# Gating tables requested behind the gate blocks, and tiles that share buffers, in a two-layer hybrid encoder

## The chip, the cores and the metric

The kernel runs on one core of one Trainium2 chip. The metric is the device time of one launch in microseconds (us), as the median of several runs. Beside it stands one profiled execution, whose instructions the hardware profiler recorded with their start, their duration and the semaphores that they waited for.

The engines have short names in the rows: PE is TensorE's matrix multiply and PEld its loading of stationary weights, DVE is VectorE, ACT is ScalarE, POOL is GpSimd, and SP is SyncE, which only issues transfers here. Each engine works off its instructions in program order.

## The reference

There are 256 tokens of width 2048 and two layers. Everything is float32.

```
for l in range(2):
    h = rms_norm(x, norm1_g[l])
    q, k, v, gu, gv = split(h @ w_in[l])                  # 1024 | 256 | 256 | 1024 | 1024
    q, k = rope(rms_norm(q per head)), rope(rms_norm(k per head))
    attn = softmax(q k^T / sqrt(128), |i-j| <= 128, learned sink) v   # 8 query heads, 2 key heads
    vn   = layer_norm(gelu(gv)) * sgu_ln_g + sgu_ln_b
    f    = w_s[head] @ vn  (per chunk of 128 tokens) + b_s
    sgu  = gelu(gu) * f
    x = x + concat(rms_norm(attn), rms_norm(sgu)) @ w_o[l]
    g, u = split(depthwise_conv3(rms_norm(x) @ w_up[l]))  # 2 x 5632
    x = x + (silu(g) * u) @ w_down[l]
```

## The kernel before

**Products.** Every float32 operand of a large product is split in two float32r parts: hi, a rounded copy that ACT makes (L128), and lo, the rest, that DVE makes by a subtraction (L112). A product is then three matmuls (hi with hi, hi with lo, lo with hi). The weights come from HBM in blocks of 128 x 2048 (1 MB), each by one transfer that SP issues (L120), into one of 3 buffers `raw`; hi and lo of half a block lie in one of 4 buffers each. A transfer into `raw` waits until DVE has made the last lo of the block that lay there, so SP runs three blocks ahead of that subtraction, and ACT and DVE run up to two blocks ahead of PE.

**Stages of a layer.** The input projection takes 20 blocks of `w_in` in chunks of 4 (keys and values, queries of head group 0, queries of head group 1, two chunks for `gv`), 24 matmuls a block (L168). Then `gu` is made in four gate units of two blocks of `w_gu` each (`unit`, 32 matmuls at L209 and 32 short ones at L214), then come `w_o`, the up projection and the down projection.

**Attention beside it.** The work of the two head groups is written as two generators (`attend`) whose steps are taken between blocks of the projection and in the gate units: a query row is scaled, squared and rotated; its rows are cut into 16-bit halves by ACT (`apart`, L422), sent through the transposing transfer (`sent`, L429, four transfers for a group, two more for the keys), put together again by ACT (`together`, L435) and split in hi and lo (`parts`, L302 and L303). Then follow the scores (`matmul3`, L308 to L310, 128 x 256), a masked reading of them by DVE (L498), exponentials on ACT (L520), the division (L528), transposes of the probabilities on PE (L536), another split and the products with the values (L308 to L310, 128 x 512). The scores and these transposes write into two PSUM buffers `tp`.

**Gating.** `gating_tables` requests eight tables of 256 KB: two of `w_s` (L408) and six rows of `prow`, each copied to all 128 partitions (L413): two of the gain, two of the offset, two of `b_s`. `normal` applies gain (L769) and offset (L770) on DVE to the normalised `gv` (L768). `spatial` multiplies with `w_s` on PE (L751) and adds `b_s` on DVE (L762).

**What sets the order.** A scheduler places each engine's instructions ahead of time. Code under `urgent()` comes as early as it can, other code in written order as its inputs are expected; `take` lets a step begin behind the latest PE instruction written so far. Most tiles, also the tables, come from one pool of 43 general buffers (`sl`), and a request waits, in the scheduler's plan and on the chip, for the last reader of what lay in its buffer. The query rows have 4 buffers `q`.

Of the kernel before, what the change touches and what calls it, by code (L numbers as in the profile page):

```python
# [8 lines left out]
F32 = mybir.dt.float32  # L9
F32R = mybir.dt.float32r  # L10
U16 = mybir.dt.uint16
AF = mybir.ActivationFunctionType
ALU = mybir.AluOpType
AX = mybir.AxisListType

P = 128
# [4 lines left out]
HD = 128  # L21
# [6 lines left out]
W = 512  # L28
# [14 lines left out]
def encoder(ctx: ExitStack, tc: tile.TileContext, xT, x, w_in, w_gu, w_o, w_up, w_down, wsT, pcol, prow, rope, out):  # L43
    nc = tc.nc
    pool = lambda name, bufs, **kw: ctx.enter_context(tc.tile_pool(name=name, bufs=bufs, **kw))
    const = pool("const", 1)
    lay = pool("lay", 2)
    slots = pool("slots", 43)
    rowp = pool("rowp", 4)
    evp = pool("evp", 4)  # L50
    rawp = pool("rawp", 3)
# [7 lines left out]
    def sl(shape, dt=F32):  # L59
        return slots.tile(shape, dt, tag="sl", name="sl")  # L60

    def row(tag):
        return rowp.tile([P, W], F32, tag=tag, name=tag)

    def ev():
        return evp.tile([P, 2, SEQ], F32, tag="ev", name="ev")
# [4 lines left out]
    def st(shape, tag):  # L71
        return small.tile(shape, F32, tag=tag, name=tag)
# [4 lines left out]
    def tp(shape):  # L77
        return tpp.tile(shape, F32, tag="tp", name="tp")
# [4 lines left out]
    def urgent():  # L83
        return tc.high_priority(offset=AHEAD)
# [215 lines left out]
    def parts(src, shape):  # L300
        hi, lo = sl(shape, F32R), sl(shape, F32R)
        nc.scalar.activation(hi, src, AF.Copy)  # L302
        nc.vector.tensor_tensor(out=lo, in0=src, in1=hi.bitcast(F32), op=ALU.subtract)  # L303
        return hi, lo
# [100 lines left out]
    def gating_tables(l):  # L405
        ws = [sl([P, 4, P]) for _ in range(2)]
        for i in range(2):
            nc.sync.dma_start(ws[i], wsT[l, :, 4 * i : 4 * i + 4, :])  # L408
        rows = []
        for r0 in (R_LG, R_LB, R_BS):  # L410
            for i in range(2):
                t = sl([P, W])
                nc.sync.dma_start(t, prow[l : l + 1, r0 + i * W : r0 + (i + 1) * W].partition_broadcast(P))  # L413
                rows.append(t)
        return ws, rows


    def apart(srcs):
        halves = []
        for src in srcs:  # L420
            h = sl([P, 2, 2 * P], U16)
            nc.scalar.copy(h, src.bitcast(U16).rearrange("p (n b) -> p b n", b=2))  # L422
            halves.append(h)
        return halves

    def sent(halves):
        tall = sl([P, 4, SEQ], U16)
        for m in range(2):
            nc.sync.dma_start_transpose(tall[:, :, m * P : (m + 1) * P], halves[m].rearrange("p b n -> p (b n)"))  # L429
        return tall  # L430

    def together(tall):
# [33 lines left out]
    def attend(g, ps, r, kT, v, tab, qk, nsink, acc, pc, outs):  # L466
        ms = st([P, 2, 4], "qms")
        rot = []
        for m in range(2):
            q = row("q")  # L470
            with urgent():
                nc.scalar.activation(q, ps[:, m, :], AF.Copy, scale=r[:, m : m + 1])
            head_squares(q, 4, ms[:, m, :])
            rot.append(rotate(q, m, 4, tab))
        qr = inv_rms(ms.rearrange("p a b -> p (a b)"), HD, "q", 8)
        qs = st([P, 8], "qs")
        nc.vector.tensor_scalar_mul(qs, qr, HD**-0.5)
        rows = [rot[m].rearrange("p h d -> p (h d)") for m in range(2)]
        halves = [apart([rows[m][:, h : h + 2 * HD] for m in range(2)]) for h in (0, 2 * HD)]
        yield  # L480
        talls = [sent(h) for h in halves]
        yield
        qT = []
        for tall in talls:
            pq = parts(together(tall), [P, 2, SEQ])
            qT += [[v[:, i, :] for v in pq] for i in range(2)]
        yield
        scores = []
        for pr in range(2):
            nmx = st([P, 2, 2], "nmx")  # L490
            for i in range(2):
                h = 2 * pr + i
                t = tp([P, 2, SEQ])
                s = sl([P, 2, SEQ])
                for m in range(2):
                    matmul3(t[:, m, :], [v[:, m * P : (m + 1) * P] for v in qT[h]], [v[:, g, :] for v in kT])
                for m in range(2):
                    nc.vector.tensor_tensor_reduce(  # L498
                        out=s[:, m, :],
                        in0=t[:, m, :],  # L500
                        in1=mask[:, m, :],
                        scale=qs[:, 4 * m + h : 4 * m + h + 1],
                        scalar=LOWEST,
                        op0=ALU.add,
                        op1=ALU.max,
                        accum_out=nmx[:, i, m : m + 1],
                    )
                scores.append(s)
            h0 = 4 * g + 2 * pr
            sink = qk[:, R_SINK + h0 : R_SINK + h0 + 2].unsqueeze(2).to_broadcast([P, 2, 2])  # L510
            nsk = nsink[:, h0 : h0 + 2].unsqueeze(2).to_broadcast([P, 2, 2])
            nm = st([P, 2, 2], "nm")
            nc.vector.scalar_tensor_tensor(out=nm, in0=nmx, scalar=-1.0, in1=nsk, op0=ALU.mult, op1=ALU.min)
            es = st([P, 2, 2], "es")
            nc.vector.tensor_tensor(out=es, in0=nm, in1=sink, op=ALU.add)
            rs = st([P, 2, 2], "rs")
            for i in range(2):
                s = scores[2 * pr + i]
                for m in range(2):
                    nc.scalar.activation(s[:, m, :], s[:, m, :], AF.Exp, bias=nm[:, i, m : m + 1], accum_out=rs[:, i, m : m + 1])  # L520
            nc.scalar.activation(es, es, AF.Exp)
            nc.vector.tensor_tensor(out=rs, in0=rs, in1=es, op=ALU.add)
            rec = st([P, 2, 2], "rec")
            nc.vector.reciprocal(rec, rs)
            for i in range(2):
                s = scores[2 * pr + i]
                for m in range(2):
                    nc.vector.tensor_scalar_mul(s[:, m, :], s[:, m, :], rec[:, i, m : m + 1])  # L528
            yield
        for pr in range(2):  # L530
            pT = []
            for b in range(2):
                t = tp([P, 2, SEQ])
                for i in range(2):
                    for m in range(2):
                        nc.tensor.transpose(  # L536
                            t[:, i, m * P : (m + 1) * P], scores[2 * pr + i][:, m, b * P : (b + 1) * P], ident
                        )
                pT.append(parts(t.rearrange("p a b -> p (a b)"), [P, W]))
            yield  # L540
            t = tp([P, W])
            for b in range(2):
                matmul3(t, [w[:, g * HD : (g + 1) * HD] for w in v[b]], pT[b], b == 0, b == 1)
            o = sl([P, 2, SEQ])
            nc.scalar.copy(o.rearrange("p a b -> p (a b)"), t)
            add_squares(acc, o, g == 0 and pr == 0)
            outs.extend(gained([o], C_AG + 4 * g + 2 * pr, pc))
            yield
# [9 lines left out]
        out=mask[:, 0, P:], in_=mask[:, 0, P:], compare_op=ALU.is_ge, fill=MASKED,  # L558
# [3 lines left out]
        out=mask[:, 1, :P], in_=mask[:, 1, :P], compare_op=ALU.is_ge, fill=MASKED,  # L562
# [60 lines left out]
    for l in range(DEPTH):  # L623
# [39 lines left out]
        kv = []  # L663
        for m in range(2):
            t = sl([P, W])
# [6 lines left out]
        for m in range(2):  # L672
            a = rotate(kv[m][:, : 2 * HD], m, 2, tabs[1])
            nc.vector.tensor_tensor(
                out=a, in0=a, in1=rk[:, 2 * m : 2 * m + 2].unsqueeze(2).to_broadcast([P, 2, HD]), op=ALU.mult
            )
            krot.append(a)
        vs = [parts(kv[m][:, 2 * HD :], [P, 2 * HD]) for m in range(2)]
        kT = []

        khalves = apart([a.rearrange("p h d -> p (h d)") for a in krot])
# [2 lines left out]
        def sent_keys():  # L684
            ktall.append(sent(khalves))
# [20 lines left out]
        r1b = as_rows(r1)  # L706
        second = group_steps(1, ps)
        second()
        ws, lrows = gating_tables(l)


        vn = []
# [1 line left out]
        for i in range(2):  # L714
            if l:
                between = [[[first], [first], [], [first]], [[first, second], [first], [second, first], [second]]]
            else:
                between = [[[first], [first], [first], [second]], [[second], [], [first], [first]]]
            ps = chunk(3 + i, between[i])
            for m in range(2):  # L720
                t = row("vn")
                with urgent():
                    nc.scalar.activation(t, ps[:, m, :], AF.Copy, scale=r1[:, m : m + 1])
                nc.scalar.activation(t, t, AF.Gelu_apprx_tanh)
                nc.vector.bn_stats(out=stats[:, m, i, :], in_=t)
                vn.append(t)
        mv = st([P, 2, 2], "mv")
        for m in range(2):
            nc.vector.bn_aggr(out=mv[:, m, :], in_=stats[:, m, :, :])
# [116 lines left out]
        for f0, f1 in ((0, 24), (24, NF)):  # L846
            ys = []
            for f in range(f0, f1, 2):
# [7 lines left out]
                t = convolved(ps2, NF + f)  # L856
# [85 lines left out]
```

## Time and profile before

| | us |
|---|---|
| median of 3 runs (lowest, highest) | 1993.09 (1992.59, 1994.17) |
| the profiled execution: its own time | 1992.69 |
| the profiled execution: span from first to last instruction | 1990.9 |
| PE busy in the span | 1985.5 |
| DVE busy, ACT busy | 1367.6, 1134.5 |

The profiled execution took 0.40 us less than the median, and 1.79 us of it lie outside the span. Matmuls are pipelined and their ends are modelled in the profile, so that PE's busy time also covers small stops; where PE stopped is read from the weight loads (PEld) that began late.

### The profile page before, as it was taken

The numbers are of one execution on the slowest core, as the hardware profiler recorded it, in microseconds if no ns is written. First come the engines' busy times: TensorE is split into PE (matmuls) and PEld (weight loads), VectorE is DVE, ScalarE is ACT, GpSimd is POOL, SyncE is SP. The second block draws the span as 40 slices with busy tenths as digits, with TensorE's granted clock in tenths as the row PEclk, the third lists the DMA queues.
The fourth block names the chain that finished last, engine by engine and source line by source line (L and its number), as shares of the span: only waits on it lengthen the run. The fifth ranks groups of instructions, "written<-read, shape, count | busy, mean of one in ns | idle before, by whom it ended". The sixth has DMA issues, their size and how long they took to land.

```text
span 1990.9 us, 26332 instructions
## 1 busy us (share of the span) xinstructions
PE 1985.5 (100%) x10292; PEld 1704.8 (86%) x10292; DVE 1367.6 (69%) x1930; ACT 1134.5 (57%) x1514; POOL 23.3 (1%) x25
## 2 busy tenths in 40 slices
PE   9999999999999999999999999999999999999999
PEld 8888888888888888888888888888888888888887
DVE  6778677777754577775566786777777445777753
ACT  6786585556543455556667675855555344555542
POOL 0100000000000000000000000000000000000000
PEclk9999999999999999999999999999999999999999
DMA  9754674455555544556767536745545554455563
GB/s 341 243 161 149 219 222 169 170 208 207 198 191 192 188 170 174 212 207 204 219 205 237 161 142 226 198 169 206 207 180 211 191 192 167 171 208 203 201 212 127
DMA packets 95580, 391.15 MB, mean 196 GB/s; under 512 B 43744, under 2 KB 45024, under 8 KB 50912
## 3 DMA queue, kind: packets, MB, share of 16 engines
q1 hardware_dynamic: 94736, 388.74, 56.6%
q8 instruction: 80, 1.31, 0.3%
q10 hardware_dynamic: 720, 0.73, 0.1%
q14 instruction: 44, 0.36, 0.1%
HBM read 378.43 MB, written 2.10 MB: 191 GB/s over the span
## 4 chain that ended last, share of the span: by engine, by line
PE 97%; ACT 1%; DVE 1%; DMA 1%; issue 0%; SPq 0%; POOL 0%; DVEq 0%; ACTq 0%
PE mm L168 42%; PE mm L234 31%; PE mm L240 16%; PE mm L209 2%; PE mm L275 1%; PE tp L168 1%; PE mm L214 1%; PE mm L270 1%; PE tp L308 0%; PE tp L751 0%; PE tp L310 0%; DVE lo L112 0%; PE tp L309 0%; DMA raw<-in_w_up 0%; ACT hi L128 0%
## 5 line engine op out<-in xcount | busy, mean ns | idle before, releaser
L112 DVE TENSOR_TENSOR lo<-raw,hi 128x1024 fp32r<-128x1024 f32 (+1 forms) x708 | 839.4, 1215 | 417.4 <-ACT hi L128 277.1
L128 ACT ACTIVATE hi<-raw 128x1024 fp32r<-128x1024 f32 (+1 forms) x708 | 730.3, 1050 | 606.8 <-PE mm L168 330.9
L168 PE MATMUL mm<-hi,sl 128*128 128x512 f32 x2480 | 667.6, 390 | 0.1
L234 PE MATMUL mm<-sl,hi 128*128 128x512 f32 x2688 | 617.8, 389 | 0.2 <-ACT hi L128 0.2
L234 PEld LDWEIGHTS mm<-sl,hi 128*128 128x128 f32 x2688 | 501.9, 188 | 103.5 <-ACT hi L128 1.1
L168 PEld LDWEIGHTS mm<-hi,sl 128*128 128x128 f32 x2480 | 464.5, 188 | 97.2 <-DVE sl L289 0.9
L168 PE MATMUL mm<-lo,sl 128*128 128x512 f32 x1240 | 382.6, 390 | 0.0
L240 PEld LDWEIGHTS mm<-sl,lo 128*128 128x128 f32 x2688 | 328.1, 192 | 3.3
L240 PE MATMUL mm<-sl,lo 128*128 128x256 f32 x2688 | 329.1, 283 | 0.0
L168 PEld LDWEIGHTS mm<-lo,sl 128*128 128x128 f32 x1240 | 232.5, 188 | 47.9
L838 DVE SCALAR_TENSOR_TENSOR sc<-ev,pc,sc 128x255 f32<-128x255 f32 x176 | 80.6, 481 | 94.0 <-ACT sc L837 94.0
L281 ACT COPY ev<-mm 128x512 f32<-128x512 f32 x96 | 55.4, 577 | 122.5 <-PE mm L240 114.8
L837 ACT ACTIVATE sc<-ev,pc 128x256 f32<-128x256 f32 x176 | 99.1, 589 | 0.0
L841 DVE SCALAR_TENSOR_TENSOR sc<-ev,pc,sc 128x255 f32<-128x255 f32 x176 | 80.6, 481 | 2.9
L296 ACT ACTIVATE sl<-sl 128x256 fp32r<-128x256 f32 x88 | 31.8, 409 | 72.8 <-DVE sl L857 72.8
L283 DVE TENSOR_TENSOR ev<-mm,ev 128x512 f32<-128x512 f32 x96 | 65.6, 683 | 0.0
L209 PE MATMUL mm<-sl,hi 128*128 128x512 f32 x256 | 61.6, 391 | 0.0
L833 DVE TENSOR_TENSOR ev<-ev,rb 128x512 f32<-128x512 f32 x88 | 60.1, 682 | 0.1
L209 PEld LDWEIGHTS mm<-sl,hi 128*128 128x128 f32 x256 | 47.3, 188 | 9.2
L289 DVE SCALAR_TENSOR_TENSOR sl<-sl,pc 128x256 fp32r<-128x256 f32 x96 | 42.6, 479 | 17.7 <-ACT sl L288 17.6
L297 DVE TENSOR_TENSOR sl<-sl 128x256 fp32r<-128x256 f32 x88 | 33.5, 422 | 19.4 <-ACT sl L296 19.4
L288 ACT ACTIVATE sl<-sl,pc 128x256 fp32r<-128x256 f32 x96 | 43.2, 497 | 1.1 <-DMA sl<-in_xT 0.9
(124 smaller groups left out, 813.2 us busy)
## 6 DMA issues: line engine op xcount, KB each, us to landing
raw<-in_w_up SPq DMA_DIRECT2D x172, 1024.0 KB, 5.2
raw<-in_w_down SPq DMA_DIRECT2D x88, 1024.0 KB, 4.9
raw<-in_w_in SPq DMA_DIRECT2D x38, 1024.0 KB, 5.1
raw<-in_w_o SPq DMA_DIRECT2D x32, 1024.0 KB, 4.9
raw<-in_w_gu SPq DMA_DIRECT2D x16, 1024.0 KB, 4.9
raw<-in_w_up SPq DMA_DIRECT2D x8, 512.0 KB, 4.5
sl<-in_prow SPq DMA_DIRECT2D x12, 256.0 KB, 7.3
raw<-in_w_in SPq DMA_DIRECT2D x8, 256.0 KB, 5.2
```

The lines of the kernel that those rows point to most:

```text
L112: nc.vector.tensor_tensor(out=lo, in0=part, in1=hi.bitcast(F32), op=ALU.subtract)
L128: nc.scalar.activation(hi[:, cs], part, AF.Copy)
L168: nc.tensor.matmul(ps[m], acts[kk][:, part % 2, m * P : (m + 1) * P], w, start=first and kk == 0 and part == 0, stop=last and kk == KB - 1 ...
L209: nc.tensor.matmul(ps[:, i, :], tile_of(his, k, i), x1, start=k == 0, stop=False)
L234: nc.tensor.matmul(pss[n][:, i, :], hs[k // KB][:, c : c + P], x1, start=k == 0, stop=False)
L240: nc.tensor.matmul(pss[n][:, i, :SEQ], los[k // KB][:, c : c + P], acts[k][:, 0, :], start=False, stop=k == len(acts) - 1)
L281: nc.scalar.copy(rest, ps[:, :, SEQ:])
L283: nc.vector.tensor_tensor(out=s, in0=ps[:, :, :SEQ], in1=rest, op=ALU.add)
L833: nc.vector.tensor_tensor(out=s, in0=s, in1=r2b2[0], op=ALU.mult)
L837: nc.scalar.activation(t[:, i, :], s[:, i, :], AF.Identity, bias=col(3), scale=col(1))
L838: nc.vector.scalar_tensor_tensor(out=t[:, i, 1:], in0=s[:, i, : SEQ - 1], scalar=col(0), in1=t[:, i, 1:], op0=ALU.mult, op1=ALU.add)
L841: nc.vector.scalar_tensor_tensor(out=t[:, i, : SEQ - 1], in0=s[:, i, 1:], scalar=col(2), in1=t[:, i, : SEQ - 1], op0=ALU.mult, op1=ALU.add)
```

## The change

Five things are changed. `gating_tables` is called behind the two `gv` chunks and no longer ahead of them. The transposing transfers of `sent` stand under `urgent()`. The hi and lo parts of a value row share one general buffer, where each had its own. The 16-bit halves of a query row for both pairs of heads are made by one ACT copy into one buffer, where there were two copies and two buffers. The query rows have 2 buffers, and the general pool has 46.

```diff
-    slots = pool("slots", 43)
+    slots = pool("slots", 46)
...
-        return rowp.tile([P, W], F32, tag=tag, name=tag)
+        return rowp.tile([P, W], F32, tag=tag, name=tag, bufs=2 if tag == "q" else 4)
...
         tall = sl([P, 4, SEQ], U16)
-        for m in range(2):
-            nc.sync.dma_start_transpose(tall[:, :, m * P : (m + 1) * P], halves[m].rearrange("p b n -> p (b n)"))
+        with urgent():
+            for m in range(2):
+                nc.sync.dma_start_transpose(tall[:, :, m * P : (m + 1) * P], halves[m].rearrange("p b n -> p (b n)"))
...
-        rows = [rot[m].rearrange("p h d -> p (h d)") for m in range(2)]
-        halves = [apart([rows[m][:, h : h + 2 * HD] for m in range(2)]) for h in (0, 2 * HD)]
+        both = []
+        for m in range(2):
+            t = sl([P, 2, 2, 2 * HD], U16)
+            words = rot[m].rearrange("p h d -> p (h d)").bitcast(U16)
+            nc.scalar.copy(t, words.rearrange("p (j n b) -> p j b n", j=2, b=2))
+            both.append(t)
+        halves = [[t[:, pr, :, :] for t in both] for pr in range(2)]
...
-        vs = [parts(kv[m][:, 2 * HD :], [P, 2 * HD]) for m in range(2)]
+        vs = []
+        for m in range(2):
+            t = sl([P, 2, 2 * HD], F32R)
+            v = kv[m][:, 2 * HD :]
+            nc.scalar.activation(t[:, 0, :], v, AF.Copy)
+            nc.vector.tensor_tensor(out=t[:, 1, :], in0=v, in1=t[:, 0, :].bitcast(F32), op=ALU.subtract)
+            vs.append([t[:, 0, :], t[:, 1, :]])
...
         second = group_steps(1, ps)
         second()
-        ws, lrows = gating_tables(l)
...
                 vn.append(t)
+        ws, lrows = gating_tables(l)
         mv = st([P, 2, 2], "mv")
```

Line numbers move: L429 becomes L430, L498 L504, L536 L542, L769 L781.

**SP, layer 0, from the first transposing transfers to the second gate unit.** Before, the tables stand between the last blocks of `w_in` and the first of `w_gu`, and the transposes of the second head group behind the third block of `w_gu`:

```order
L429 DMA_TRANSPOSE sl<-sl 128x4x128 x5
L120 DMA raw<-in_w_in 128x2048
L429 DMA_TRANSPOSE sl<-sl 128x4x128
L120 DMA raw<-in_w_in 128x2048 x2
L408 DMA sl<-in_wsT 128x512 x2
L413 DMA sl<-in_prow 128x512
L120 DMA raw<-in_w_in 128x2048
L413 DMA sl<-in_prow 128x512 x2
L120 DMA raw<-in_w_gu 128x2048
L413 DMA sl<-in_prow 128x512 x3
L120 DMA raw<-in_w_gu 128x2048 x2
```

and now all eight tables stand in one piece behind the fifth block of `w_gu`:

```order
L430 DMA_TRANSPOSE sl<-sl 128x4x128 x6
L120 DMA raw<-in_w_in 128x2048 x4
L430 DMA_TRANSPOSE sl<-sl 128x4x128 x4
L120 DMA raw<-in_w_gu 128x2048 x5
L408 DMA sl<-in_wsT 128x512 x2
L413 DMA sl<-in_prow 128x512 x6
L120 DMA raw<-in_w_gu 128x2048 x3
```

The tables moved behind five weight blocks and the transposes of group 1 ahead of all blocks of `w_gu`. In layer 1 the tables also stand behind the fifth block of `w_gu`.

**DVE, layer 0, the gain and offset.** Before, the gain (L769) comes one row at a time, between other small work, when the gate units run:

```order
L768 TENSOR_SCALAR vn<-vn,mv,lnr 128x512
L513 SCALAR_TENSOR_TENSOR nm<-nmx,nsink 128x4
L768 TENSOR_SCALAR vn<-vn,mv,lnr 128x512
L515 TENSOR_TENSOR es<-nm,qk 128x4
L769 TENSOR_TENSOR vn<-vn,sl 128x512
L303 TENSOR_TENSOR sl<-tp,sl 128x512
L770 TENSOR_TENSOR vn<-vn,sl 128x512
L769 TENSOR_TENSOR vn<-vn,sl 128x512
```

and now the gain stands ahead of the four score readings (L504) of head group 1, which free the two buffers `tp`, and of the next lo parts (L112):

```order
L743 TENSOR_SCALAR lnv<-mv 128x2
L780 TENSOR_SCALAR vn<-vn,mv,lnr 128x512 x4
L781 TENSOR_TENSOR vn<-vn,sl 128x512 x3
L504 ISA sl,nmx<-tp,mask,qs 128x256
L504 ISA nmx 128x1
```

The first two instructions of L781 read the first row of `prow` and the third reads the second row. In layer 1 DVE's order is alike, with these three instructions ahead of two score readings, the division and four lo parts.

**PE, layer 1, the first gate units.** Before, the value products of group 0 (L308 to L310, 128x512) and its scores of group 1 (128x256) stand inside the first units:

```order
L209 MATMUL mm<-sl,hi 128x512 x32
L214 MATMUL mm<-sl,lo 128x256 x10
L308 MATMUL tp<-sl 128x512
L309 MATMUL tp<-sl 128x512
L310 MATMUL tp<-sl 128x512
L308 MATMUL tp<-sl 128x512
L214 MATMUL mm<-sl,lo 128x256 x4
L309 MATMUL tp<-sl 128x512
L310 MATMUL tp<-sl 128x512
L214 MATMUL mm<-sl,lo 128x256 x8
L308 MATMUL tp<-sl 128x256
L309 MATMUL tp<-sl 128x256
```

and now group 0 is through before the units begin, and a unit and a half lie between the last scores of group 1 (the first row) and what follows on them (L542):

```order
L310 MATMUL tp<-sl 128x256
L214 MATMUL mm<-sl,lo 128x256 x30
L209 MATMUL mm<-sl,hi 128x512 x32
L214 MATMUL mm<-sl,lo 128x256 x2
L542 MATMUL tp<-ident,sl 128x128 x8
L214 MATMUL mm<-sl,lo 128x256 x30
L209 MATMUL mm<-sl,hi 128x512 x24
```

The steps of attention stand in whole groups of 6, 8 or 12 now, at the places where they are written. Over both layers PE has the same instructions as before; its order differs only from the first scores to the products with `w_o` in each layer. ACT loads its function tables 14 times in the program, and did so 17 times before.

## Rows read from the trace of the kernel before

**Rows 1.** The page: span, share of the engines, and the clock granted to PE in 40 equal slices (9 is 90% or more of full speed).

```profile
span 1990.9 us, 26332 instructions
PE 1985.5 (100%) x10292; PEld 1704.8 (86%) x10292; DVE 1367.6 (69%) x1930; ACT 1134.5 (57%) x1514; POOL 23.3 (1%) x25
...
PEclk9999999999999999999999999999999999999999
```

**Rows 2.** The chain of work that ended last, in order of time: start in us, duration in us, what; 64 long and 64 short matmuls of the up projection.

```profile
312.62 14.53 PE mm L234 x64
327.15 7.67 PE mm L240 x64
```

**Rows 3.** Waits of the weight loads in layer 0 from 74.91 to 208.93 us, grouped: who waited for whom, us in total, times, longest.

```profile
PEld tp L308 <- issue: 0.8, 2, 0.6
PEld tp L336 <- issue: 0.5, 1, 0.5
PEld mm L168 <- DVE sl L289: 0.4, 1, 0.4
PEld tp L536 <- DVE sl L528: 0.3, 1, 0.3
PEld tp L536 <- ACT sl L545: 0.2, 1, 0.2
PEld mm L168 <- ACT sl L288: 0.2, 1, 0.2
```

**Rows 4.** The same view of layer 1, from 1064.36 to 1196.53 us.

```profile
PEld mm L168 <- DVE sl L289: 0.6, 2, 0.4
PEld tp L310 <- DVE sl L303: 0.5, 1, 0.5
PEld tp L536 <- ACT sl L545: 0.5, 2, 0.3
PEld tp L536 <- DVE sl L528: 0.4, 2, 0.2
PEld tp L308 <- DVE nmx L498: 0.4, 1, 0.4
PEld tp L308 <- DVE sl L303: 0.3, 1, 0.3
PEld tp L308 <- ACT sl L302: 0.2, 1, 0.2
PEld tp L308 <- ACT sl L545: 0.2, 1, 0.2
```

**Rows 5.** The time line of the weight loads, those that began late: start, duration, instruction, and in brackets the idle time before and what ended it. The first two are of layer 0, the last four of layer 1.

```profile
115.94 0.47 PEld L536 LDWEIGHTS tp<-ident,sl 128*128 128x128 f32 x4 [0.34 <-DVE sl L528]
126.58 0.19 PEld L308 LDWEIGHTS tp<-sl 128*128 128x128 f32 x1 [0.59 <-issue]
...
1093.41 0.19 PEld L308 LDWEIGHTS tp<-sl 128*128 128x128 f32 x1 [0.35 <-DVE nmx L498]
...
1106.98 0.19 PEld L308 LDWEIGHTS tp<-sl 128*128 128x128 f32 x1 [0.34 <-DVE sl L303]
1110.69 0.42 PEld L536 LDWEIGHTS tp<-ident,sl 128*128 128x128 f32 x4 [0.32 <-ACT sl L545]
...
1130.46 0.19 PEld L310 LDWEIGHTS tp<-sl 128*128 128x128 f32 x1 [0.54 <-DVE sl L303]
```

**Rows 6.** Busy time (and instructions) of PE, PEld, DVE, ACT and POOL, granted clock, DMA share and GB/s in two stretches of layer 0.

```profile
113.00:119.00 6.00, 6.00 (x32) 4.75 (x30) 4.55 (x12) 5.95 (x14) 0.00 (x0) 1.00 0.89 230
119.00:127.00 8.00, 7.80 (x35) 6.20 (x34) 3.90 (x7) 7.58 (x10) 0.00 (x0) 1.00 0.45 155
```

**Rows 7.** The time line of SP in layer 0: start, time that the queue took for the issues, line, what, how many.

```profile
69.31 6.55 SPq L429 DMA_TRANSPOSE sl<-sl  x5
...
87.06 0.90 SPq L408 DMA_DIRECT2D sl<-in_wsT  x2
...
95.90 0.33 SPq L120 DMA_DIRECT2D raw<-in_w_gu  x1
```

**Rows 8.** All issues of rows of `prow`: duration of the issue in ns (least, median, most), first and last start; and for all transfers from `prow`, with two of another kind, the time from issue to landing in us. The third row is the page's: size of a block of `w_gu` and its median time to landing.

```profile
L413 SPq DMA_DIRECT2D sl<-in_prow x12: 338/436/2047, 88.0 to 1087.2; - x12
...
DMA to landing us min/median/max: 4.5/7.1/9.9
...
raw<-in_w_gu SPq DMA_DIRECT2D x16, 1024.0 KB, 4.9
```

**Rows 9.** Durations by line and shape, over the whole span: instructions, busy us, mean ns of one, idle us before them.

```profile
L128 ACT ACTIVATE hi<-raw 128x1024 fp32r<-128x1024 f32 x700 | 725.2, 1055 | 604.7 <-PE mm L168 330.9 <-issue 184.8 <-DVE lo L112 18.7
L435 ACT COPY sl<-sl 128x1024 uint16<-128x1024 uint16 x10 | 13.5, 1352 | 0.7 <-DMA sl<-sl 0.7
L302 ACT ACTIVATE sl<-sl 128x512 fp32r<-128x512 f32 x10 | 6.3, 633 | 0.3
...
L112 DVE TENSOR_TENSOR lo<-raw,hi 128x1024 fp32r<-128x1024 f32 x700 | 834.0, 1221 | 415.2 <-ACT hi L128 275.0 <-PE mm L240 107.7 <-issue 26.2
L498 DVE CUSTOM_DVE_ANT_0 sl<-tp,mask,qs 128x256 f32<-128x256 f32 x32 | 14.0, 478 | 0.2 <-PE tp L310 0.2
L528 DVE TENSOR_SCALAR sl<-sl,rec 128x256 f32<-128x256 f32 x32 | 9.1, 348 | 0.2
L769 DVE TENSOR_TENSOR vn<-vn,sl 128x512 f32<-128x512 f32 x8 | 5.5, 688 | 0.0
```

## The prediction

> **What bounds the kernel now.** I read the page first. PE is busy for 1985.5 of 1990.9 us and DVE and ACT for 69% and 57%, and PE's clock is granted in full in all 40 slices, which is the level of 2.4 GHz [rows 1]. So the kernel is bound by PE, and only time in which PE stands still can be won. The reader must not take 1990.9 - 1985.5 for that time, because the modelled ends cover short stops. The chain of waits shows what PE does when nothing holds it: 64 long matmuls in 14.53 us and 64 short ones in 7.67 us, so 0.227 and 0.120 us each [rows 2]. The up and down projections run at this pace for most of the span, and the change leaves their order alone.
>
> Next I looked for the stops where the change works, between the first scores and the products with `w_o`. The waits of the weight loads show them: 0.8 + 0.5 + 0.4 + 0.3 + 0.2 + 0.2 = 2.4 us in layer 0 [rows 3], and 0.6 + 0.5 + 0.5 + 0.4 + 0.4 + 0.3 + 0.2 + 0.2 = 3.1 us in layer 1 [rows 4]. Together they are 5.5 us, 0.28% of the time. This is the most that any better order of these steps can give back. Each stop is short (0.59 us at most), and its releaser is a computation of DVE or ACT, not a transfer or a weight block. The time line says where the largest ones are: at the transposes and value products of group 0 (115.94, 126.58 and 1106.98 us), and around the scores of group 1 (1093.41 and 1130.46 us, with 1110.69 between them) [rows 5]. There ACT works for 5.95 of 6.00 and for 7.58 of 8.00 us [rows 6]: the attention steps come late and in a heap, on top of the gate units' own splitting.
>
> A measurement of this kernel can tell about 0.2%, or 4.0 us, from no change.
>
> **The change, part by part.** *Fewer and shared buffers.* Two general buffers fewer are asked for the values and four for the query halves of a layer, three more exist, and the tables no longer take eight of them while group 0 needs them. The result in the order is that group 0's steps move up to where they are written. Of the stops, six lie at the steps that move: 0.34 + 0.59 + 0.35 + 0.34 + 0.32 + 0.54 = 2.48 us [rows 5]. If all move to a place with room, 2.5 us are won; if they only reappear elsewhere, nothing. In layer 1 the steps now stand 24 or more matmuls apart (5.4 us and more), while a split takes 0.63 us on ACT and a subtraction of that shape 0.69 on DVE [rows 9], so I take 1.9, three quarters. The other 3.0 us belong to steps behind them (the row sums, `spatial`, the splits ahead of `w_o`), which stay about where they are.
>
> *The first scores of layer 0* now stand 63 weight matmuls (14.3 us) earlier. In ACT's order a weight copy, the joining copy and the split come right ahead of them; the weight copy waits for a buffer that PE frees 14 matmuls earlier. 13 matmuls remain after that, 2.95 us, and the three ACT instructions take 1.06 + 1.35 + 0.63 = 3.04 us [rows 9]. With some 0.3 us for the matmul's end and the semaphores PE waits 0.4 us. The bounds are nothing, since before the change the same chain stood ahead of these scores and of the two waits of L308 in layer 0 the one near them took 0.2 us, the other 0.6 elsewhere [rows 3], and 1.1 us, if the first score also waits for the subtraction (0.69 us).
>
> *The tables.* This is the change's new wait. The fifth block of `w_gu` is issued when DVE has subtracted the second, which it can do as soon as the last `gv` block is through. I put that at 0.3 us behind the first unit's start: 1.22 us for the subtraction [rows 9], against about 1.4 us of attention matmuls that PE does in between. Behind it SP needs 0.33 us for the block, 0.90 for two tables of `w_s` [rows 7] and about 0.44 for the first row of `prow` [rows 8], so the second row is asked 1.7 us later. Rows took 4.5 to 9.9 us to land, with a median of 7.1 [rows 8]. The least is excluded, since the block ahead takes 4.9 us itself [rows 8] and two tables and a row follow. I take a landing 10 us behind the block's issue, between 8.8 (median) and 11.6 (most), and in the middle because now everything comes in one piece. Behind the waiting L781 on DVE stand the score readings that free the two buffers `tp`.
>
> In layer 0 the row is there 10.3 us after the unit's start; the third gain (0.69) and four readings (4 x 0.48) end at 12.9 us [rows 9]. PE comes to the transposes after 32 long and 44 short matmuls: 7.26 + 5.28 = 12.5 us, and the second four of them need the last reading about 0.4 us later. The wait is 0.2 us at most; call it 0.2. In layer 1 the gain (0.69), four readings (1.9), four divisions (4 x 0.35), four lo parts (4 x 1.22), two additions (2 x 0.69) and small ones (0.3) end at 10.3 + 10.6 = 20.9 us [rows 9]. PE needs them after 64 long and 46 short matmuls, at 14.53 + 5.5 = 20.0, or 20.4 for the second four: 0.5 us. Together 0.7 us; nothing if the rows land with the median, and 1.6 us more in each layer, 3.9 us, with the longest landing. The rows of the offset and of `b_s` are read behind some 9 us more of DVE's work, so they have room.
>
> *The transposes ahead of the weights.* Five of them held SP for 6.55 us, 1.3 each [rows 7]. Six in one piece take 7.9 us, so a weight block is issued at most 1.3 us later than before, and the four of group 1 hold SP for 5.2 us elsewhere. The cover is the lead: three blocks for SP and up to two for ACT and DVE. A block is 24 x 0.227 = 5.4 us of PE, and it lands in 4.9 us [rows 8], so about 10 us are to spare. The price is nothing; if that cover were used up, it would be 1.3 us for a block. The copies of the query halves and the table loads that ACT saves cost or give nothing by themselves, since PE waits for neither; they are in the 1.9 us.
>
> *Sum.* -1.9 + 0.4 + 0.7 = -0.8 us. The profiled execution took 1992.69 us, 1990.9 in the span and 1.79 around it, so it would take 1991.9; it lies 0.4 under the median, so I predict **1992.3 us**.
>
> **The rivals.** *The tables come too late* (the other side). The mechanism is DVE's wait at L781 with the readings behind it. What speaks for it: the eight requests are one piece now, and DVE holds no other work ahead of the readings. What speaks against it: no row of the trace shows DVE idle ahead of the gain (0.0 us at L769, rows asked long before) [rows 9], and the sum above has the need and the landing within half a microsecond of each other. With the longest landing seen the sum is -1.9 + 0.4 + 3.9 = +2.4, 1995.5 us. Each microsecond beyond that costs two, one a layer. From 12.4 us after the block's issue on, the kernel is slower by 4 us: 1997.1. The Trainium skill, "DMA: Bandwidth & Descriptors", Rules for kernel authors, speaks for this rival: "Issue the DMA early, do compute, wait on its semaphore late". The change does the contrary; by that rule it loses, and the trace agrees so far that tables asked early were never waited for.
>
> *All stops go.* If lack of buffers is behind every stop in these stretches, 5.5 us are won and nothing is added: 1993.1 - 5.5 = 1987.6. The Trainium skill, "Perfetto Trace Analysis", Optimization Strategy, reads bubbles that repeat on the engine that should be full as a sign that SBUF ran out for the next tile. The trace bears it out only in part: the stops come at irregular distances, and they are ended by computations [rows 3, 4].
>
> *No difference.* The stops move with the steps: what group 0 no longer suffers, group 1 does, since now its exponentials and divisions share the gate units with the gains and offsets. Then the time is 1993.1.
>
> **How the numbers follow.** I give the forecast 0.62 (1990.6 to 1994.0, with the stops that go between 0.9 and 2.5 and the tables between nothing and 1.6), no difference 0.16, late tables 0.16, half of it beyond 1997.1, and the vanishing of all stops 0.06. So faster by over 0.2% (below 1989.1) has 0.06, slower (above 1997.1) 0.08, and the rest is 0.86. The range 1989.8 to 1996.2 leaves out the last rival, the worse half of the late tables and some 0.04 of the tails.
>
> **What would show it.** In the changed profile the weight loads' waits in layer 1's first units should be nearly gone, with at most two behind L504 or L534. DVE should stand idle for some 3 to 6 us ahead of the first L781 in each layer, ended by a transfer from `prow`, and the PE stop behind it at the transposes L542 should be under 1 us. In layer 0 a stop of about 0.4 us should stand at the first scores, at about 88 us. SP should show six transposes in a row with no stop of PE after them. The prediction is wrong if PE stops for more than 2 us behind L781, if weight blocks arrive late behind the tables or transposes, or if the stops at the end of the gate units grow, which I took as fixed.

## The result and the profile after

The changed kernel is slower, by about as much as a measurement can tell.

| | before | changed |
|---|---|---|
| median of 16 runs each (lowest, highest) | 1992.33 (1991.27, 1994.17) | 1997.13 (1993.49, 2001.60) |
| ratio, 95% interval | | 1.0022 [1.0015, 1.0030] |
| the profiled execution: own time, span | 1992.69, 1990.9 | 1997.32, 1995.4 |

I predicted 1992.3, between 1989.8 and 1996.2. Not only the median moved: the runs of the changed kernel spread over 8.1 us, those before over 2.9. With each run goes its mean granted clock of TensorE. It is 1.000 in every run of the kernel before that was made beside the experiments. In the changed kernel it is 1.000 in 4 of 16 runs (1993.5 to 1994.6 us) and 0.999 to 0.997 in the other 12 (1994.9 to 2001.6 us).

The page of the changed kernel answers to [rows 1]. In its slices of 50 us nothing is to be seen of the clock.

```profile
span 1995.4 us, 26320 instructions
...
PE 1984.3 (99%) x10292; PEld 1705.8 (85%) x10292; DVE 1367.5 (69%) x1930; ACT 1129.8 (57%) x1503; POOL 21.7 (1%) x25
...
PEclk9999999999999999999999999999999999999999
```

The waits of the weight loads of the changed kernel, from 60 to 1230 us (who waited for whom, us in total, times, longest), answer to [rows 3, 4].

```profile
PEld tp L308 <- ACT sl L302: 3.6, 1, 3.6
PEld tp L308 <- DVE nmx L504: 2.7, 1, 2.7
PEld tp L308 <- issue: 0.7, 2, 0.4
PEld tp L308 <- PE mm L209: 0.4, 1, 0.4
PEld tp L309 <- DVE sl L303: 0.4, 1, 0.4
```

Two long stops, 3.6 and 2.7 us, have come. Besides them only 1.5 us stand here, and four more waits of 0.2 us each in layer 0, so 2.3 us where there were 5.5 before (both are sums of rounded rows). The gate units are nearly clean, as predicted.

**The first stop, layer 0.** The time line of ACT (start, duration, instruction, idle time before and what ended it):

```profile
78.17 1.35 ACT L436 COPY sl<-sl 128x1024 uint16<-128x1024 uint16 x1 [2.11 <-DMA sl<-sl]
79.55 0.63 ACT L302 ACTIVATE sl<-sl 128x512 fp32r<-128x512 f32 x1
...
85.69 1.05 ACT L483 COPY sl<-sl 128x1024 uint16<-128x1024 uint16 x1 [2.37 <-DVE sl L454]
87.09 1.05 ACT L483 COPY sl<-sl 128x1024 uint16<-128x1024 uint16 x1 [0.35 <-DVE sl L454]
88.05 1.05 ACT L128 ACTIVATE hi<-raw 128x1024 fp32r<-128x1024 f32 x1
89.00 1.32 ACT L436 COPY sl<-sl 128x1024 uint16<-128x1024 uint16 x1
90.35 0.63 ACT L302 ACTIVATE sl<-sl 128x512 fp32r<-128x512 f32 x1
```

PE has come to group 0's first scores at 87.7 us and begins them at 91.03, when the last of these instructions gives them their hi part. The join of the queries (L436 at 89.00) had nothing to wait for: the last of the six transposes landed at 79.54 us. It stood behind the two 16-bit copies of head group 1 (L483), and these waited 2.37 and 0.35 us for DVE's rotation of group 1 (L454).

**The second stop, layer 1.** The time line of DVE:

```profile
1076.90 0.16 DVE L323 TENSOR_SCALAR qv<-qms 128x8 f32<-128x8 f32 x1
1077.02 0.69 DVE L454 TENSOR_TENSOR sl<-sl 128x512 f32<-128x512 f32 x1
1079.24 0.17 DVE L478 TENSOR_SCALAR qs<-qr 128x8 f32<-128x8 f32 x1 [1.53 <-POOL qr L325]
1079.32 0.48 DVE L504 CUSTOM_DVE_ANT_0 sl<-tp,mask,qs 128x256 f32<-128x256 f32 x1
...
1079.72 1.22 DVE L112 TENSOR_TENSOR lo<-raw,hi 128x1024 fp32r<-128x1024 f32 x1
1080.86 0.48 DVE L504 CUSTOM_DVE_ANT_0 sl<-tp,mask,qs 128x256 f32<-128x256 f32 x1
```

The second pair's scores need a buffer `tp`, which the readings L504 of the first pair free. On DVE these stand behind group 1's whole rotation, and behind its scale (L478), which waits 1.53 us for a power that POOL computes. PE begins at 1081.40.

**The clock.** Busy time (and instructions) of PE, PEld, DVE, ACT and POOL, granted clock, DMA share and GB/s around that stop:

```profile
1078.00:1081.40 3.40, 1.15 (x6) 0.61 (x5) 2.16 (x7) 3.03 (x3) 1.21 (x1) 1.00 0.00 0
1081.40:1086.00 4.60, 4.60 (x19) 3.99 (x20) 3.98 (x17) 0.60 (x2) 0.00 (x0) 0.65 0.66 228
1086.00:1092.00 6.00, 6.00 (x27) 4.91 (x27) 3.56 (x8) 4.99 (x15) 0.00 (x0) 0.99 0.30 75
```

PE is busy for 1.15 of 3.40 us, and in the 4.6 us behind it the granted clock is 0.65 on average, partly at the lower level of 1.2 GHz (from 1083 to 1086 us it is 0.50). That costs 0.35 x 4.6 = 1.6 us. The first stop of this execution was not followed by a fall: the granted clock is 1.00 from 91 to 100 us.

So the sum after the fact is: +3.6 and +2.7 for the two stops, -3.2 for the stops that went (5.5 to 2.3), +1.6 for the clock, 4.7 us. The two profiled executions differ by 4.6. That it closes so well is partly luck, since the waits of the weight loads outside these stretches grew by another 0.6 us.

**What had little or no price.** The gain L781 in layer 0 and in layer 1, SP's first requests for tables in both layers, and SP at the six transposes:

```profile
132.99 1.90 DVE L781 TENSOR_TENSOR vn<-vn,sl 128x512 f32<-128x512 f32 x3 [0.60 <-DMA sl<-in_prow]
1129.41 1.92 DVE L781 TENSOR_TENSOR vn<-vn,sl 128x512 f32<-128x512 f32 x3 [2.16 <-DMA sl<-in_prow]
```

```profile
125.21 0.89 SPq L408 DMA_DIRECT2D sl<-in_wsT  x2
...
1121.59 0.90 SPq L408 DMA_DIRECT2D sl<-in_wsT  x2
```

```profile
69.95 8.36 SPq L430 DMA_TRANSPOSE sl<-sl  x6
78.40 10.15 SPq L120 DMA_DIRECT2D raw<-in_w_in  x3
```

The tables are asked for 34 and 40 us after the two long stops have ended (91.03 and 1081.40 us), so their landing cannot be behind these. DVE waits 0.60 and 2.16 us for the tables, and PE shows no wait of 0.2 us or more in the 19 us after that. One way to PE exists all the same. In layer 1 the last products with the values wait 0.4 us (the list above puts that down to PE itself), and in a second profile of this kernel (e11 below) 0.7 us. There the chain of waits leads back from them to a table:

```profile
1125.20 7.80 DMA sl<-in_prow
...
1134.85 2.28 DVE lo L112 x2
...
1137.18 4.87 DMA raw<-in_w_gu
...
1144.18 1.28 ACT L526
...
1151.69 0.60 DVE sl L303
...
1152.44 0.47 PE tp L308
```

DVE's lo parts come late behind the gain, so the next weight block goes out late, so ACT's exponentials and the split behind them are late. With the tables asked early the same products waited 1.0 us (e2) and 0.7 (e10), so a price of the late tables is not shown; the longest wait at the end of such a chain is 0.9 us (e1).

At the transposes the weight block behind them goes out at 78.40 us, and PE waits for no block in this stretch.

### The profile page after: what moved, and what is told of

The parts are those of the page before. It is cut to its first block, busy times and chain, and to the rows that moved or that the text cites. A ratio compares the mean times of both kernels' runs of the same rounds, so it can differ in the third digit from the quotient of the medians.

```text
span 1995.4 us, 26320 instructions
## 1 busy us (share of the span) xinstructions
PE 1984.3 (99%) x10292; PEld 1705.8 (85%) x10292; DVE 1367.5 (69%) x1930; ACT 1129.8 (57%) x1503; POOL 21.7 (1%) x25
## 4 chain that ended last, share of the span: by engine, by line
PE 96%; DVE 1%; DMA 1%; ACT 0%; issue 0%; SPq 0%; POOL 0%; DVEq 0%; ACTq 0%; POOLq 0%
PE mm L168 40%; PE mm L234 30%; PE mm L240 16%; PE mm L209 3%; PE mm L214 2%; PE mm L275 1%; PE tp L168 1%; PE mm L270 1%; DVE lo L112 1%; DMA sl<-sl 0%; PE tp L308 0%; PE tp L763 0%; DMA raw<-in_w_up 0%; PE tp L309 0%; PE tp L542 0%; PE tp L310 0%
## 5 line engine op out<-in xcount | busy, mean ns | idle before, releaser
L112 DVE TENSOR_TENSOR lo<-raw,hi 128x1024 fp32r<-128x1024 f32 (+1 forms) x708 | 839.7, 1214 | 430.9 <-ACT hi L128 286.1
L168 PE MATMUL mm<-hi,sl 128*128 128x512 f32 x2480 | 666.2, 390 | 0.3 <-ACT hi L128 0.3
L168 PEld LDWEIGHTS mm<-hi,sl 128*128 128x128 f32 x2480 | 465.0, 188 | 96.8 <-ACT hi L128 1.0
L168 PE MATMUL mm<-lo,sl 128*128 128x512 f32 x1240 | 383.5, 390 | 0.0
L168 PEld LDWEIGHTS mm<-lo,sl 128*128 128x128 f32 x1240 | 233.0, 188 | 48.7 <-DVE lo L112 0.3
L289 DVE SCALAR_TENSOR_TENSOR sl<-sl,pc 128x256 fp32r<-128x256 f32 x96 | 42.5, 479 | 17.7 <-ACT sl L288 17.7
L288 ACT ACTIVATE sl<-sl,pc 128x256 fp32r<-128x256 f32 x96 | 43.3, 497 | 0.8 <-DMA pc<-in_pcol 0.6
```

The lines of the kernel that those rows point to most:

```text
L112: nc.vector.tensor_tensor(out=lo, in0=part, in1=hi.bitcast(F32), op=ALU.subtract)
L168: nc.tensor.matmul(ps[m], acts[kk][:, part % 2, m * P : (m + 1) * P], w, start=first and kk == 0 and part == 0, stop=last and kk == KB - 1 ...
```

## The experiments

The theory is: steps of group 0 that the change moved forward stand in line on ACT and DVE behind work of group 1 that nobody needs yet. Its rivals are the shared buffers, weight blocks held up by the transposes, and the place on PE as such. All ratios are to runs of the kernel before on the same chip, made beside them. Waits are those of the weight loads, from 60 to 1230 us.

| | median | ratio, 95% interval | runs below a mean clock of 1.000 |
|---|---|---|---|
| e1 tables only | 1994.57 | 1.0010 [1.0001, 1.0019] | 4 of 11 |
| e2 tables back | 1992.66 | 1.0000 [0.9991, 1.0009] | 0 of 11 |
| e3 not urgent | 1995.24 | 1.0015 [1.0006, 1.0024] | 9 of 11 |
| e4 scores later | 1991.89 | 0.9997 [0.9988, 1.0005] | 0 of 11 |
| e5 layer 0 later | 1995.76 | 1.0012 [1.0003, 1.0021] | 7 of 11 |
| e6 layer 1 later | 1994.71 | 1.0008 [1.0000, 1.0017] | 5 of 11 |
| e7 folded scale | 1994.22 | 1.0007 [0.9997, 1.0016] | 7 of 11 |
| e8 rotation later | 1990.86 | 0.9985 [0.9976, 0.9994] | 0 of 11 |
| e9 e8 and e7 | 1990.16 | 0.9988 [0.9979, 0.9997] | 0 of 11 |
| e10 e8, tables back | 1991.57 | 0.9994 [0.9985, 1.0002] | 0 of 11 |
| e11 changed again | 1997.39 | 1.0024 [1.0014, 1.0034] | 8 of 8 |

**e1: the tables alone.** The kernel before, with one line moved.

```diff
         second()
-        ws, lrows = gating_tables(l)
...
                 vn.append(t)
+        ws, lrows = gating_tables(l)
```

> The kernel before, with nothing changed but the place where the tables are requested. My theory is that this line alone moves group 0's scores forward (in PE's order they stand within 0.5 us of where the changed kernel has them) and that they come too early for ACT and DVE: a stop of 2.5 to 3.5 us at the first scores of layer 0, one of 2 to 3 us at the second pair's scores of layer 1, 1995.5 to 1999 us and a wide spread. A rival has the loss come from the shared buffers or from the transposes put first: then this kernel takes 1991.5 to 1993.5 us, as the one before.

The two longest waits (the readings L504 are L498 in these lines):

```profile
PEld tp L308 <- DVE nmx L498: 3.0, 1, 3.0
PEld tp L308 <- ACT sl L302: 1.8, 1, 1.8
```

Both stops are there, the first smaller than expected and the time 1 us under my range. The slowest run of before (1993.58) lies under the fastest of this kernel (1993.70). So the table line alone moves the scores and brings both stops; the buffers and the transposes are not needed for that. But by the medians it makes only 2.1 us of loss, where the whole change makes 4.8 (the two intervals still overlap a little). The other four changes seem to add the rest, and only together with this line, as e2 shows. One part of it is the first stop, 3.6 us in place of 1.8.

**e2: the tables back.** The changed kernel with the same line moved the other way.

> The changed kernel with the tables requested where they were. By my theory the scores of layer 0 stand 13.6 us later again and the second pair's of layer 1 10.9 us later, so both stops go: 1991 to 1993.5 us, with a spread under 3 us. By the rival (shared buffers, transposes ahead of the weights) it stays at 1996 to 1998 us.

1992.66 us, as before, spread 2.0. The two stops are gone: the wait on L302 is 0.6 us, that on L504 0.2, and no wait is over 1.0. This is the counter-test of e1: without the table line the other four changes cost nothing.

**e3: the transposes without `urgent`.**

```diff
-        with urgent():
-            for m in range(2):
...
+        for m in range(2):
...
```

> The changed kernel without the urgent mark on the transposing transfers. One instruction moves in each layer at most: the last of six transposes of layer 0 goes behind one weight block; the keys' stay first and fourth. My theory expects the stop at the first scores to stay (2.3 to 4.3 us) and the time at 1996 to 1998 us. A rival, that weight blocks held up behind six transposes cause the loss, expects the stop to shrink by 1.3 us or more and a time below 1995.5 us.

The wait on L302 is 2.1 us, that on L503 (the readings) 2.8, the time 1995.24. My range was missed and the rival's numbers came in, yet the chain of waits names no weight transfer. From the scores it leads back over ACT's copies L483 (L482 here) and DVE's rotation of group 1, as in the changed kernel; there it goes on to the keys' transpose, here it does not. So some 2 us of the stop stand behind the rotation alone, and a late transpose adds to them. What differs is when the fourth transpose, the keys' second, landed: 76.97 us against 78.09 in the changed kernel. The mark alone does not decide this: in e6, with six in one piece, it landed at 77.39 (wait 2.3), in e11 at 78.22 (wait 3.6), in e1, again without the mark, at 76.58 (wait 1.8). But it may make a late landing more frequent. Without the mark the fourth transpose took 2.7 to 3.1 us from issue to landing in all three profiles (before, e1, e3). With six in one piece it took 2.7 to 2.9 us in four profiles (e4, e6, e9, e10) and 4.1 to 4.7 in six (the changed kernel, e11, e2, e5, e7, e8). So the run doesn't settle whether the mark costs something of its own, by way of the keys; the intervals of e3 and e11 overlap.

**e4: group 0's scores one block later.** The first pair of lines is layer 1, the second layer 0.

```diff
-                between = [[[first], [first], [], [first]], [[first, second], [first], [second, first], [second]]]
+                between = [[[first], [], [first], [first]], [[first, second], [first], [second, first], [second]]]
...
-                between = [[[first], [first], [first], [second]], [[second], [], [first], [first]]]
+                between = [[[first], [], [], [first, second]], [[second, first], [], [first], [first]]]
```

> The changed kernel with the scores of group 0 written one block of the projection later: both pairs in layer 0 (first scores 5.7 us further on PE than in the changed kernel), the second pair alone in layer 1 (2.5 us further). My theory, that they merely stand too early for ACT and DVE, expects both stops to fall under 0.5 us and the time to be 1989 to 1991.5 us, faster than the kernel before, spread under 3 us. If the stops only move to the transposes and products behind the scores, 1992 to 1995 us. If the tables or the transposes cause the loss, 1996 us or more.

```profile
PEld tp L542 <- DVE nmx L504: 0.9, 1, 0.9
PEld tp L309 <- DVE sl L303: 0.7, 1, 0.7
```

Both stops at the scores are gone and the profiled execution took 1989.96 us, but the median is 1991.89, 0.4 over my range and not to be told from before: part of the waiting comes back at the probabilities (L542).

**e5 and e6: the same in one layer each.** e5 takes the two lines for layer 0, e6 those for layer 1.

> The changed kernel with the scores of group 0 one block later in layer 0 alone; layer 1 as changed. The stop at the first scores of layer 0 should be under 0.5 us and the one at the second pair's scores of layer 1 (about 1076 us) still 2.0 to 2.8 us, so 1993 to 1995 us. This and the next kernel also tell which stop is followed by the fall of TensorE's clock. My theory, from the changed kernel's profile, is that of layer 1: then some runs here have a mean granted clock of 0.999 or less. The rival is that of layer 0, or both: then all runs here are at 1.000.

> The changed kernel with the second pair's scores later in layer 1 alone; layer 0 as changed. The stop of layer 1 should be under 0.5 us, that of layer 0 stays at 1.5 to 3.3 us: 1992.5 to 1994.5 us. All runs at a granted clock of 1.000 if the fall follows on layer 1's stop alone; some at 0.999 or less if it follows on layer 0's too.

In e5 the wait of layer 1 stays (2.8 us) and that of layer 0 is gone from the scores; 2.8 us in three waits on L504 at L542 have come for it (0.9 in e4, with the same order). The longest, 1.5 us, follows on a late transpose of group 1, which took 5.45 us in the chain. The time, 1995.76, lies 0.8 us over my range. In e6 the wait of layer 0 stays at 2.3 us and that of layer 1 is 0.4; the time, 1994.71, lies 0.2 over the range. On the clock my theory was wrong: both kernels have runs below 1.000. In e6 the fall follows on layer 0's stop:

```profile
88.00:91.00 3.00, 1.16 (x8) 0.71 (x6) 1.92 (x2) 2.97 (x4) 0.00 (x0) 1.00 0.83 262
91.00:95.00 4.00, 4.00 (x16) 3.56 (x15) 3.08 (x9) 2.08 (x3) 0.00 (x0) 0.57 0.50 119
```

**e7: the scale folded into the power.**

```diff
...
-        qr = inv_rms(ms.rearrange("p a b -> p (a b)"), HD, "q", 8)
-        qs = st([P, 8], "qs")
-        nc.vector.tensor_scalar_mul(qs, qr, HD**-0.5)
+        qs = inv_rms(ms.rearrange("p a b -> p (a b)"), 1, "q", 8, eps=EPS * HD)
```

> The changed kernel without the DVE instruction that multiplies the query's scale by 1/sqrt(128); the constant goes into the sum that POOL raises to the power -1/2. The order on PE, ACT and SP is the same; DVE loses four instructions, two of which stood idle for 1.53 us on POOL, with the rotation (layer 0) or the score readings (layer 1) behind them. By my theory both stops shrink by about 1.5 us: to 0.4 to 1.8 us in layer 0 (more where the keys' transposes land late) and 0.5 to 1.0 us in layer 1, 1991 to 1993.5 us, and falls of the clock are rare. By the rival, that these stops come from DVE's own load of work and the POOL wait is hidden, nothing changes: 1995 to 1998 us.

```profile
PEld tp L308 <- ACT sl L302: 4.0, 1, 4.0
PEld tp L308 <- DVE nmx L502: 0.6, 1, 0.6
```

In layer 1 the wait falls from 2.7 to 0.6 us, with the order on PE unchanged: DVE's wait for POOL was on the path. In layer 0 it doesn't fall, and the time line of ACT shows why.

```profile
79.20 1.35 ACT L436 COPY sl<-sl 128x1024 uint16<-128x1024 uint16 x1 [2.57 <-DMA sl<-sl]
```

The keys' last transpose landed at 79.12 us here, and the rotation on DVE stands behind the keys' lo part (L303), which waited 3.62 us. Two waits in front of the same line hide each other; to take one away wins only what the other leaves. So the time, 1994.22, missed my range by 0.7 us, and the falls of the clock were not rare (7 of 11 runs).

**e8: group 1's rotation later.** The line of layer 0 is changed in the same way.

```diff
...
+        if g:
+            yield
+        for m in range(2):
+            head_squares(qrows[m], 4, ms[:, m, :])
+            rot.append(rotate(qrows[m], m, 4, tab))
...
-                between = [[[first], [first], [], [first]], [[first, second], [first], [second, first], [second]]]
+                between = [[[first], [first, second], [], [first]], [[first, second], [first], [second, first], [second]]]
```

> The changed kernel with squares, rotation and 16-bit copies of head group 1 taken one step later (behind the block after the first pair's scores), so that nothing of group 1 stands ahead of group 0's scores on DVE and ACT. The scheduler puts the first scores of layer 0 another 5.2 us earlier, and the second pair's of layer 1 another 2.9 us. My theory, that the stops come from standing in line behind group 1's rotation, expects them to shrink in spite of that: to at most 1.5 us in layer 0 and 0.5 in layer 1, 1990.5 to 1993 us. The rival, that the place on PE alone is to blame (the transposes and joins cannot be ready so early, whatever else stands in line), expects the stop of layer 0 to grow to 5 us or more and 1996 us or more.

```profile
PEld tp L308 <- ACT sl L302: 1.6, 2, 1.2
PEld tp L308 <- issue: 0.5, 2, 0.3
PEld tp L310 <- DVE sl L303: 0.4, 1, 0.4
```

```profile
1069.55 1.21 DVE L112 TENSOR_TENSOR lo<-raw,hi 128x1024 fp32r<-128x1024 f32 x1
1070.68 0.48 DVE L509 CUSTOM_DVE_ANT_0 sl<-tp,mask,qs 128x256 f32<-128x256 f32 x1
```

The first lines are the waits of the weight loads, the others DVE's time line: the readings (L509 here) begin at 1070.68 us, in the changed kernel at 1079.32, and the wait of 2.7 us is gone. In layer 0 the first scores begin at 83.6 us in place of 91.0 and wait 1.2 us in place of 3.6, though the keys' transpose landed as late as 78.58. This decides against the place on PE as such. The kernel is faster than the changed one and than the one before: 0.9985 of the time before.

**e9: both together.**

> The kernel with the later rotation and, in addition, the scale folded into POOL's operand as in the experiment on it. The places on PE are those of the later rotation. There the stop at the first scores of layer 0 hung on ACT's joining copy and split and not on DVE, so by my theory the folded scale adds little: 0 to 0.7 us, 1989 to 1991 us, clock at 1.000 in all runs. If the wait of DVE for POOL is still ahead of the readings, it gives 1.5 us or more.

1990.16 us. The profile has no wait over 0.4 us between 60 and 1230 us; but the keys' transpose landed at 77.22, 1.4 us earlier than in e8's profile, so that I don't credit the scale with it. By the ratios e8 and e9 are equal.

**e10: the rotation later, the tables back.**

> The kernel with the later rotation, but with the tables requested where the kernel before has them. It tells what moving the tables is worth once nothing of group 1 stands in line. If early scores of group 0 are a gain of their own, as I first predicted (1.9 us), this kernel takes 1992 to 1993 us, 1 to 2 us more than with the tables moved. If the later rotation alone makes the gain, it takes 1990 to 1991.5 us as well.

1991.57 us lies between both expectations, and its interval overlaps those of e8 and e9. Whether the moved tables gain 1 to 2 us once the line is free stays open.

**e11: the changed kernel again.**

> The changed kernel once more, beside the two others. 1994.5 to 1997.5 us; the runs with a granted clock of 1.000 at 1993.5 to 1995 us and each thousandth of the mean clock less adding about 2 us. Stops of 1.9 to 3.7 us at the first scores of layer 0, by when the keys' last transpose lands (76.6 to 79.1 us in the profiles so far), and of 2.3 to 2.8 us in layer 1.

1997.39 us, waits of 3.6 and 2.7 us, and here the clock falls behind layer 0's stop, for longer:

```profile
92.00:98.00 6.00, 6.00 (x21) 5.11 (x21) 3.44 (x10) 1.94 (x3) 0.00 (x0) 0.56 0.51 167
```

0.44 x 6 = 2.6 us. No run was at 1.000.

## Why the prediction was wrong

**What bounds the kernel** was right: PE, and its stops. But I took the full clock in [rows 1] as given. The forecast had no term for what a longer stop does to it. One reading was wrong too: not every stop of before was ended by a computation of DVE or ACT. For 1.3 of the 5.5 us the rows name no engine ("issue"), the longest of 0.59 us among them [rows 3].

**The stops that go** (-1.9): the mechanism held, the term was too small. The lists give -3.2, and 1.1 us of that are waits of L168 for L288 and L289, splits that I took as fixed.

**The first scores of layer 0** (+0.4, bounds 0 and 1.1): this step failed; it measured 3.6. I let the chain begin with the weight copy, held by a buffer of PE's, and added 1.06 + 1.35 + 0.63. The trace has these three in a row (88.05 to 90.98), as the sum said, but not held by PE: one place ahead of them stand the two copies L483, and DVE's rotation, for which these wait, had itself stood behind the scale (1.53 us for POOL) and the keys' lo part (another 1.34 us for a late transpose). I had read ACT's order only back to the first instruction that waits for PE and never asked what group 1's copies wait for. The Trainium skill, "Perfetto Trace Analysis", Tensor Engine Instruction, says that "ACT/DVE/GPSIMD are strict FIFO". The trace agrees: ACT stood idle for 2.37 us at L483 with a ready join behind it. The upper bound of 1.1 came from the chain that I had, so it bounded nothing.

**The second pair in layer 1** (no term): 2.7 us. "24 or more matmuls apart" is a distance on PE. The work that stands between the two pairs on DVE is what counts: the rotation and the 1.53 us at L478. e7 and e8 show both.

**The tables** (+0.7): nothing that could be measured. The mechanism is there: the second row landed 9.2 us behind the fifth block's issue in layer 0 and 9.3 in layer 1, where I took 10. I expected DVE idle for 3 to 6 us; it was 0.60 and 2.16, since DVE was itself later, with 0.81 us for a power on POOL ahead of it. The rival of late tables, on whose side the result fell, is not what made the loss: both long stops end before a table is asked for, and the one way from a table to PE that the chains show ends in waits of 0.7 (e11) and 0.9 us (e1). That way leads over a late weight block, and not over the buffers `tp`, as I had it. The Trainium skill, "DMA: Bandwidth & Descriptors", Rules for kernel authors, would have kept this kernel from the loss with its early issue, but not for the reason that it gives, that "the fixed setup cost overlaps". Here the early request held back group 0's steps in the order (e1 and e2 show that the line does it; that it does so through the buffers is my reading of the code).

**The transposes ahead of the weights** (0): right for the weight blocks (8.36 us against the 7.9 that I took). I left out that the transposes themselves are waited for: the first stop is longer where the keys land late, 1.8 us at 76.58 (e1) and 3.6 at 78.09.

**The clock** (no term): 1.6 us in the profile. For the median it is more: the four runs at 1.000 have a median of 1994.4, 2.0 over the kernel before, and the median of all is 4.8 over it. So about 2 us are the stops, less what was won, and about 2.8 what the clock adds. That is an account over few runs, and the four may be those with the shorter stops; only the profiled falls are seen directly.

**All stops go** came nearer than I thought: 3.2 of 5.5 us went, and in e8 and e9, without the line, the kernel is 2 to 3 us faster than before.

## To carry to other kernels

When a scheduler pulls a step forward, read every in-order engine that the step passes through, back past the first wait that you expect, and price whatever else waits in that line, above all work of a later group that nobody needs yet. A step that comes earlier in the order is no gain in itself: here consumers moved ahead into a line that had not moved, and the cure was to hold back the producer that was not needed. Price a stop of 2 us and more on PE above its length.

## What the runs showed of the hardware

The mean granted clock was below 1.000 in 52 of 79 runs of the six kernels whose profile has a stop of 2 us or more (the changed kernel, run twice, e1, e3, e5, e6, e7). It was below in none of the 55 runs of e2, e4, e8, e9 and e10, and in none of the kernel before that was made beside them. It isn't the length alone: in the profiles the clock fell after waits of 2.3 us (e6, layer 0), 2.7 (changed, layer 1), 3.6 (e11, layer 0) and 4.0 (e7, layer 0), and not after 2.7 (e11, layer 1), 2.8 (e3 and e5, layer 1), 3.0 (e1, layer 1) or 3.6 (changed, layer 0).

A transposing transfer at the same place landed 2.7 to 4.7 us after its issue: the fourth of layer 0 was issued between 73.5 and 74.6 us and landed between 76.58 and 79.12 in the profiles of the changed kernel and the experiments.

A power on 128 x 8 numbers took POOL 2.0 to 2.6 us, four times in the profile of the changed kernel, and DVE stood still for 1.53 us each time.
